# The work beside the experts begins at rank 16 in place of 4 and ends at 59, and until rank 16 five more places hold loaded weights

## The chip, the core and the metric

The kernel runs on one core of a Trainium2 chip. The metric is the device time of one execution in microseconds (us). A core has TensorE (PE in the profile; PEld is its weight load), VectorE (DVE), ScalarE (ACT), GpSimd (POOL) and SyncE (SP), each with its own queue of instructions that it takes in order, and 16 DMA engines that all queues share.

## The reference, cut to what matters

One decoder layer for 520 tokens (512 of a prompt, 8 samples), 1024 wide, in float32. The part that the change touches is the mixture of experts: 64 experts, each token goes to 8 of them, beside them a shared expert and a gated per-layer input.

```python
def moe(x, w):
    scores = sigmoid(xf @ w_router);  top 8 of scores + router_bias;  gates = 2.5 * top_s / sum(top_s)
    for each expert e, for its tokens tok with gates g:
        h = silu(xb @ w1[e]) * (xb @ w3[e])          # 1024 -> 256
        acc[tok] += (h @ w2[e]) * g                  # 256 -> 1024
    shared = (silu(xf @ ws1) * (xf @ ws3)) @ ws2
    return acc + shared

x  = layer_norm(ALPHA * x + mixer(x))
ff = moe(x, w)
ple = sigmoid(x @ w_ple_gate) * (p_l @ w_ple)
x  = layer_norm(ALPHA * x + ff + ple)
```

## The kernel before, in words

The first third of the program is the mixer (projections, state-space branch, attention); the change doesn't touch it. `second_phase` then does the first norm, the router, and the experts.

**Ranks.** The router sorts the experts by load; rank 0 is the first expert handled, and `CAPS` gives the most rows of each rank, from 112 down to 56. The loop `for e in range(NE + 1)` (L1597) handles one rank a turn. It issues the input product of rank e (`expert_in`, 24 matmuls of 512 columns), the transposes of the rows of rank e+1 (`turn`), the output product of rank e-1 (`expert_out`, 12 matmuls of 512 columns, then the gate on ScalarE, L1448, and a scatter that adds the rows into one of two sums in DRAM, L1449), and `fetch(e + 3)`: the row numbers of rank e+3 and the gather of its rows (L1412). Odd ranks below 58 add into the second sum (`accD` with the higher number in the order), all others into the first. At the end of rank 60 and 61 `second_sums` (L1374) adds the second sum to the residual by five accumulating DMAs that GpSimd issues.

**Weights.** An expert's weights are six pieces of 512 KB. `Stream.load_to` (L307) issues their DMAs on SyncE (L318) in the order in which they are used, into places for loaded weights: a piece takes a place until it has been split. `Stream.split_to` splits it into a high part (ScalarE, L269, `hi`) and a rest (`lo`, L265, on VectorE, on GpSimd for one piece in six). A product then takes three matmuls: high by high, high by rest, rest by high. There are seven places for good (`raw2`, tag "raw2", RAW2 = 7). `stream.use(n, ...)` says from which piece on which pool gives the places. Until rank 4 pieces also go to five places of the pool `pre` (PRE = 5), in turns of seven and five.

**The work beside the experts.** The list `side` (L1595) has 39 steps: six for the second half of the shared expert's input (`shared_more`), six for its output (`shared_out`), four times six for the per-layer input (`layer_inputs`: a step that loads weights, then one of 30 matmuls of 256 columns for each of five tiles of tokens), and three for the last norm's scales. Their tiles are named `x` (the PSUM bank), `ph`, `pl` (the split weights), `praw` (the one place into which these weights are loaded, L1313 on SyncE) and `pt`. They need the pool `pw`, which is opened where `pre` is closed (L1618 to L1620). The `while` (L1621) says at which rank a step is issued: step n when (e - 4) * 39 / 52 reaches n, so from rank 6 to 56.

**Order.** Within this the order on each engine is the program's own scheduler's: it moves instructions between neighbouring steps as far as their tiles allow.

Of the kernel before, what the change touches and what calls it, by code (L numbers as in the profile page):

```python
# [46 lines left out]
RAW2 = 7  # L47
YB = 2
PRE = 5
VB = 5  # L50
N_SIDE = 39
SECOND = 58
SIDE = N_SIDE / 52
N_DENSE = 54
assert len(CAPS) == NE

# [144 lines left out]
def trunk_step(ctx: ExitStack, tc: tile.TileContext, I, O):  # L201
# [29 lines left out]
    def open_pool(*a, **k):  # L231
        cm = pool(*a, **k)
        p = cm.__enter__()
        opened.append((p, cm))
        return p
# [109 lines left out]
    P2 = 48  # L345
# [26 lines left out]
    stream = Stream(srcs)  # L372
# [364 lines left out]
    side = []  # L737
# [536 lines left out]
    def shared_mid(out, hg):  # L1274
        S.activation(hg, out[:, 0:128], AF.Silu)
        mul(V, hg, hg, out[:, 128:256])
        return hg

    def shared_turn(hg, i, c):

        ps = bank()
        T.transpose(ps[:, 0:TT], hg, ident[0:TT, 0:TT])
        split(H['shared'][:, i, 0, c], H['shared'][:, i, 1, c], ps[:, 0:TT])

    def shared_in():

        pair = [mm2(), mm2()]
        outs = [pair[i // 2][0:TT, i % 2] if i < 4 else psx.tile([128, 512], F32, tag="x", name="x")[0:TT] for i in R5]
        outs = [o[:, 0:256] for o in outs]
        for q in range(2):  # L1290
            hi, lo = (t.rearrange("p (k n) -> p k n", k=4) for t in stream.get(P2 + q, 0))
            for i in R5:
                yield from shared_product(outs[i], i, hi, lo, range(4 * q, 4 * q + 4), 4 * q)
        H['first half'] = outs
# [111 lines left out]
    def fetch(e):  # L1406
        find(e)
        gather(e)
# [18 lines left out]
    def expert_in(e):  # L1427
        ps, m = bank(), CAPS[e]
        for q in range(4):
            hi, lo = (t.rearrange("p (k n) -> p k n", k=2) for t in stream.get(AT[e] + q))  # L1430
            ffn_in(ps[0:m], *XT[e], hi, lo, q, slice(0, m))
        HG[e] = ffn_mid(ps, m)
        XT.pop(e)
# [41 lines left out]
    def second_phase():  # L1475
# [5 lines left out]
        raw2 = open_pool("raw2")  # L1481
# [69 lines left out]
        moe = open_pool("moe", side="right")  # L1551
        stream.use(P2, None, (moe, "v", VB))
        pre = open_pool("pre", side="right")
        stream.use(P2 + RAW2, (pre, "pre", PRE))
        stream.use(P2 + RAW2 + PRE, (raw2, "raw2", RAW2))
        stream.use(P2 + 2 * RAW2 + PRE, (pre, "pre", PRE))
        stream.use(P2 + 2 * RAW2 + 2 * PRE, (raw2, "raw2", RAW2))
        filler = shared_in()

        def fill(n):  # L1560
# [34 lines left out]
        side = [(q, i) for q in range(-2, 4) for i in range(-1, 5)]  # L1595
        side += [(4, -1), (4, 0), (4, 1)]
        for e in range(NE + 1):  # L1597
            if e == NE - 1:
                last_rows()
            if 0 < e < NE:  # L1600
                expert_in(e)
            if 0 < e < NE - 1:
                turn(e + 1)
            if e:
                expert_out(e - 1)
            else:
                H['shared'] = py.tile([128, 5, 2, 2, TT], F32R, tag="side", name="st")
                mids = py.tile([MAX_CAP, 1024], F32, tag="y", bufs=YB, name="mids")
                mids = [shared_mid(H['first half'][i], mids[0:TT, 128 * i:128 * i + 128]) for i in R5]
            if 0 < e < 6:  # L1610
                shared_turn(mids[e - 1], e - 1, 0)
            if 0 < e < NE - 1:
                HT[e] = ffn_turn(HG.pop(e), CAPS[e])
            if e + 3 < NE:
                fetch(e + 3)
            for i in {SECOND + 2: (0, 1, 2), SECOND + 3: (3, 4)}.get(e, ()):
                second_sums(i)
            if e == 4:  # L1618
                close_pool(pre)
                pw = open_pool("pw")  # L1620
            while side and (e - 4) * SIDE >= N_SIDE - len(side) + 1:  # L1621
                q, i = side.pop(0)
                if q == -2:
                    shared_more(i)
                elif q == -1:
                    shared_out(i)
                elif q < 4:
                    layer_inputs(q, i)
                else:
                    last_scales(i)  # L1630
# [66 lines left out]
    def last_rows():  # L1697

        yy = pw.tile([128, 2, 1024], F32R, tag="pl", name="yy")
        H['yh'], H['yl'] = yy[:, 0], yy[:, 1]  # L1700
        to = H['to'] = pw.tile([128, 5, TT], F32R, tag="praw", name="to")
        G.memset(yy.bitcast(F32), 0.0)
        G.memset(to.bitcast(F32), 0.0)
        for e in (NE - 2, NE - 1):
            m, z = CAPS[e], 64 * (NE - 1 - e)
            oh = OH.pop(e)
            for tiles in ((0, 1, 2), (3, 4)):
                ps = mm2()[:, 0]
                for n, i in enumerate(tiles):
                    T.matmul(ps[z:z + m, TT * n:TT * n + TT], lhsT=oh[:, i], rhs=ident_b[0:TT, 0:TT], start=True, stop=True)  # L1710
                a, b = tiles[0], tiles[-1] + 1
                S.activation(to[z:z + m, a:b], ps[z:z + m, 0:TT * len(tiles)].rearrange("p (i t) -> p i t", t=TT), AF.Copy)
# [116 lines left out]
    close_pool(gpool)  # L1829
    close_pool(qkv)  # L1830
    second_phase()


# [16 lines left out]
```

## Time and profile before

| what | value |
|---|---|
| median of three runs | 1328.86 us (1328.29 to 1329.45) |
| profiled execution: time, span | 1326.8 us, 1325.1 us |
| busy in the span: PE, DVE, ACT, POOL | 1188.6, 939.5, 700.4, 535.2 us |
| expert ranks 4 to 62 | 504.21 to 1284.94 us |

The profile is of one execution. Its span runs from the first to the last instruction. A rank is counted here from the start of its SiLU on ScalarE (L1254, the tile `hg`) to that of the next rank; the stretches in the rows are cut at these starts, which are 504.21 us for rank 4, 677.04 for rank 16, 855.59 for rank 29, 1156.44 for rank 54, 1237.15 for rank 60 and 1284.94 for rank 63. Matmuls are pipelined: a row's duration is longer than the distance to the next start, which is what a matmul costs in a stream of them. The DMA share is the busy share of the 16 DMA engines, and q1 is the queue of the weights, q0 that of the gathers, scatters and accumulating DMAs.

### The profile page before, as it was taken

To read this page: it belongs to the slowest core of one execution; us is meant where nothing else is said; L and a number is where in the kernel's file an instruction comes from. 1 tells how busy PE (TensorE), PEld (TensorE's weight loads), DVE (VectorE), ACT (ScalarE), POOL (GpSimd) and SP (SyncE) were. 2 spreads that over 40 slices of the span, in tenths; PEclk is the share of its full clock that TensorE was granted. 3 is DMA by queue.
4 is the path that set the end of the run, shared out by engine and by line. 5 is a ranking of instruction groups with operands and counts; after the bars stand their busy time and mean duration, and the time that the engine had idled before them with its cause. 6 is when DMAs were issued, how large, how long until landed. Compare 5 with 4: busy or idle time off the path is not lost. (4 is left out here: it accounts for less than half of the span.)

```text
span 1325.1 us, 20407 instructions
## 1 busy us (share of the span) xinstructions
PE 1188.6 (90%) x7083; PEld 887.7 (67%) x7084; DVE 939.5 (71%) x1397; ACT 700.4 (53%) x1055; POOL 535.2 (40%) x327
## 2 busy tenths in 40 slices
PE   7699999999998979888899888899999999988683
PEld 7699799899877856556566566667666666644341
DVE  7974657833468778576779566788877887766566
ACT  4131535222213566566567556677767776766462
POOL 1822141011124446343656335454554544455325
PEclk9897899999997989888999889999999999989897
DMA  8476563253343699889989978999999999979973
GB/s 295 124 255 114 188 202 121 83 143 96 112 149 103 196 266 252 255 264 294 310 253 322 299 232 280 286 335 318 332 319 309 335 318 293 291 254 279 256 218 93
DMA packets 114236, 312.93 MB, mean 236 GB/s; under 512 B 37041, under 2 KB 37465, under 8 KB 113055
## 3 DMA queue, kind: packets, MB, share of 16 engines
q1 hardware_dynamic: 68307, 247.11, 54.8%
q0 software_dynamic: 30848, 43.33, 15.0%
q10 hardware_dynamic: 14974, 21.14, 6.0%
q8 instruction: 57, 0.93, 0.3%
q14 instruction: 50, 0.41, 0.1%
HBM read 276.32 MB, written 32.87 MB: 233 GB/s over the span
## 5 line engine op out<-in xcount | busy, mean ns | idle before, releaser
L265 DVE TENSOR_TENSOR lo<-raw,hi 128x1024 fp32r<-128x1024 f32 x371 | 519.1, 1410 | 197.9 <-ACT hi L269 193.2
L269 ACT ACTIVATE hi<-raw 128x1024 fp32r<-128x1024 f32 x434 | 450.4, 1055 | 259.6 <-DMA raw<-in_we_dram 107.2
L1449 POOL DMA_INDIRECT accD<-y,idx x62 | 127.4, 2054 | 283.0 <-ACT hh L269 146.9
L210 PE MATMUL a<-hi,xgh 128*64 128x512 f32 (+18 forms) x512 | 212.7, 415 | 7.0 <-ACT hi L269 4.8
L210 PE MATMUL a<-lo,xgh 128*64 128x512 f32 (+18 forms) x512 | 210.8, 412 | 5.2 <-DVE lo L265 5.0
L210 PE MATMUL a<-hi,xgl 128*64 128x512 f32 (+18 forms) x512 | 207.6, 405 | 0.0
L265 POOL TENSOR_TENSOR lo<-raw,hi 128x1024 fp32r<-128x1024 f32 x63 | 169.7, 2694 | 54.2 <-ACT hi L269 45.2
L1412 POOL DMA_INDIRECT xg<-xD,idx x64 | 114.1, 1783 | 104.6 <-DVE idx L1394 43.2
L210 PE MATMUL mm<-xh,hi 128*128 128x260 f32 (+1 forms) x576 | 120.5, 290 | 18.9 <-DVE r L259 10.5
L210 PE MATMUL mm<-xl,hi 128*128 128x260 f32 (+1 forms) x576 | 119.1, 288 | 0.7 <-DVE xl L265 0.7
L210 PE MATMUL mm<-xh,lo 128*128 128x260 f32 (+1 forms) x576 | 119.1, 288 | 0.0
L210 PEld LDWEIGHTS a<-hi,xgh 128*64 128x64 f32 (+18 forms) x512 | 75.9, 148 | 51.8 <-ACT hi L269 8.5
L210 PEld LDWEIGHTS a<-lo,xgh 128*64 128x64 f32 (+18 forms) x512 | 76.1, 149 | 45.2 <-DVE lo L265 10.4
L210 PEld LDWEIGHTS mm<-xh,hi 128*128 128x128 f32 x576 | 91.3, 193 | 19.8 <-issue 10.8
L210 PEld LDWEIGHTS a<-hi,xgl 128*64 128x64 f32 (+18 forms) x512 | 75.6, 148 | 38.4 <-issue 4.5
L210 PE MATMUL mm<-lo,hh 128*64 128x512 f32 (+18 forms) x256 | 86.2, 419 | 15.1 <-POOL lo L265 12.5
L210 PEld LDWEIGHTS mm<-xl,hi 128*128 128x128 f32 x576 | 91.0, 193 | 1.3 <-DVE xl L265 1.0
L210 PE MATMUL mm<-hi,hh 128*64 128x512 f32 (+18 forms) x256 | 85.5, 416 | 7.1 <-ACT hi L269 6.7
L210 PEld LDWEIGHTS mm<-xh,lo 128*128 128x128 f32 x576 | 91.2, 193 | 0.1
L1448 ACT ACTIVATE y<-mm,both 78x1024 f32<-78x1024 f32 (+19 forms) x62 | 68.7, 1107 | 36.1 <-PE mm L210 33.0
L210 PE MATMUL mm<-hi,hl 128*64 128x512 f32 (+18 forms) x256 | 83.6, 409 | 0.0
L215 PEld LDWEIGHTS a<-ident,xg 64*128 64x128 f32 (+18 forms) x512 | 50.9, 146 | 43.1 <-issue 16.8
(410 smaller groups left out, 1971.4 us busy)
## 6 DMA issues: line engine op xcount, KB each, us to landing
raw<-in_we_dram SPq DMA_DIRECT2D x384, 512.0 KB
raw<-in_wd_dram SPq DMA_DIRECT2D x50, 512.0 KB
accD<-zeros_b POOLq DMA_DIRECT2D x2, 2560.0 KB
praw<-in_wp_dram SPq DMA_DIRECT2D x8, 512.0 KB
base<-in_xtok_dram ACTq DMA_DIRECT2D x1, 2080.0 KB
xD<-base ACTq DMA_DIRECT2D x5, 416.0 KB
base<-accD POOLq DMA_DIRECT2D x5, 416.0 KB
acc<-accD SPq DMA_DIRECT2D x5, 416.0 KB
```

What stands on the lines that cost most here:

```text
L210: ins = nc.tensor.matmul(*a, **k)
L215: ins = nc.tensor.transpose(*a, **k)
L265: return e.tensor_tensor(out=o, in0=a, in1=b, op=ALU.subtract)
L269: a = S.activation(hi, src, AF.Copy)
L1412: G.indirect_dma_start(out=XG[e % 3][0:m], out_offset=None, in_=xD[:, :], in_offset=bass.IndirectOffsetOnAxis(ap=IX[e][0:m, 0:1], axis=0), ...
L1448: S.activation(y.rearrange("p (h n) -> p h n", h=2), ps[0:m], AF.Copy, scale=GC.pop(e)[0:m])
L1449: G.indirect_dma_start(out=sumsD[e % 2 if e < SECOND else 0][:, :], out_offset=bass.IndirectOffsetOnAxis(ap=IX.pop(e)[0:m, 0:1], axis=0), ...
```

## The change

Three things. The steps of `side` are issued from rank 18 to 59: step n when (e - 16) * 39 / 43 reaches n. The pool `pre` is closed, and `pw` opened, at rank 16. And the turns of seven and five places go on until then: pieces 55, 67, 79, 91, 103, 115 and 127 each begin five in `pre`, where before only the first two did; from piece 132 on all go to `raw2`. Since a line is added ahead of it, lines L53 to L1553 have numbers higher by one in the changed kernel.

```diff
-SIDE = N_SIDE / 52
+ALONE = 16
+SIDE = N_SIDE / 43
...
-        stream.use(P2 + RAW2, (pre, "pre", PRE))
-        stream.use(P2 + RAW2 + PRE, (raw2, "raw2", RAW2))
-        stream.use(P2 + 2 * RAW2 + PRE, (pre, "pre", PRE))
-        stream.use(P2 + 2 * RAW2 + 2 * PRE, (raw2, "raw2", RAW2))
+        for n in range(P2 + RAW2, P2 + 6 * ALONE - PRE, RAW2 + PRE):
+            stream.use(n, (pre, "pre", PRE))
+            stream.use(n + PRE, (raw2, "raw2", RAW2))
...
-            if e == 4:
+            if e == ALONE:
                 close_pool(pre)
                 pw = open_pool("pw")
-            while side and (e - 4) * SIDE >= N_SIDE - len(side) + 1:
+            while side and (e - ALONE) * SIDE >= N_SIDE - len(side) + 1:
```

What this moves on TensorE, at rank 5 (92 rows). Before, the rank's output product (`mm`) is followed by the first step of the side work, matmuls from `ph` and `pl` into `x`:

```order
L210 MATMUL mm<-hi,hl 94x512 x2
L215 MATMUL a<-ident,mids 128x104
L210 MATMUL x<-ph,x1h 104x256
L210 MATMUL x<-pl,x1h 104x256
L210 MATMUL x<-ph,x1l 104x256
```

In the changed kernel the next rank's input product (88 rows) follows at once:

```order
L211 MATMUL mm<-hi,hl 94x512 x2
L211 LDWEIGHTS oh
L211 MATMUL x<-what,oh 84x6
...
L216 MATMUL a<-ident,mids 128x104
L216 MATMUL a<-ident,hg 128x92 x2
L211 MATMUL a<-hi,xgh 88x512
L211 MATMUL a<-lo,xgh 88x512
```

So the 24 matmuls of that step are gone from rank 5. The number of side matmuls by rank follows from the same order (36 matmuls of 512 columns belong to each rank itself). Ranks 4 to 15: 120 of 256 columns and 12 of 512 before, none now. Ranks 16 to 28: 150 of 256 and 48 of 512 before; 120 and 24 now. Ranks 29 to 53: 450 of 256 before; 480 of 256 and 36 of 512 now, in columns as much as 552 of 256. Ranks 54 to 59: four of 512 before; 120 of 256 and two of 512 now. On SyncE the first load of side weights stands behind 29 expert loads before, behind 89 now.

What moves on GpSimd near the end of the experts. Before, the five accumulating DMAs of the second sum (L1374) come behind the gathers of the last two ranks (the last `xg` row) and behind the scatter of rank 57 (`accD_148`) and that of rank 58 (`accD_147`):

```order
L1412 DMA xg_4187<-xD,idx 56x1024
L1449 DMA accD_147<-y,idx 640x1024
L265 TENSOR_TENSOR lo<-raw,hi 128x1024
L1412 DMA xg_4189<-xD,idx 56x1024
L1449 DMA accD_148<-y,idx 640x1024
L1412 DMA xg_4185<-xD,idx 56x1024
L265 TENSOR_TENSOR lo<-raw,hi 128x1024
L1449 DMA accD_147<-y,idx 640x1024
L1374 DMA base<-accD_148 104x1024 x5
```

In the changed kernel they come right behind the scatter of rank 57, ahead of the scatter of rank 58 and of the gather of rank 62; the gather of rank 63 is the last row here:

```order
L1450 DMA accD_148<-y,idx 640x1024
L266 TENSOR_TENSOR lo<-raw,hi 128x1024
L1375 DMA base<-accD_148 104x1024 x5
L1450 DMA accD_147<-y,idx 640x1024
L266 TENSOR_TENSOR lo<-raw,hi 128x1024
L1413 DMA xg_4189<-xD,idx 56x1024
L1702 MEMSET yy 128x2048
L266 TENSOR_TENSOR lo<-raw,hi 128x1024
L1450 DMA accD_147<-y,idx 640x1024
L1413 DMA xg_4185<-xD,idx 56x1024
```

So the five accumulating DMAs moved ahead of one scatter and of the gathers of the last two ranks, which stood ahead of them.

## Rows read from the trace of the kernel before

**Rows 1.** The page: busy times, then tenths of the span's 40 slices.
```profile
PE 1188.6 (90%) x7083; PEld 887.7 (67%) x7084; DVE 939.5 (71%) x1397; ACT 700.4 (53%) x1055; POOL 535.2 (40%) x327
...
PEclk9897899999997989888999889999999999989897
DMA  8476563253343699889989978999999999979973
```

**Rows 2.** Stretches by rank: busy us (instructions), granted clock, DMA share.
```profile
core 0: us, PE busy (x) PEld busy (x) DVE busy (x) ACT busy (x) POOL busy (x), PEclk, DMA share, GB/s
504.21:677.04 172.83, 148.41 (x771) 102.92 (x770) 123.33 (x166) 103.31 (x147) 82.61 (x38) 0.91 0.90 276
677.04:855.59 178.55, 158.87 (x856) 107.22 (x855) 131.61 (x180) 113.27 (x153) 82.33 (x40) 0.94 0.92 285
855.59:1156.44 300.85, 295.26 (x1711) 197.62 (x1710) 247.63 (x334) 216.17 (x299) 152.62 (x75) 1.00 0.99 317
1156.44:1237.15 80.71, 71.18 (x325) 36.27 (x325) 52.23 (x71) 49.35 (x70) 41.32 (x21) 0.94 0.85 266
1237.15:1284.94 47.79, 36.67 (x141) 17.72 (x142) 28.36 (x27) 25.39 (x37) 16.18 (x11) 0.82 0.83 235
```

**Rows 3.** DMA, 504.21 to 677.04: packets, MB, share of 16 engines; then issues.
```profile
q1 hardware_dynamic: 10742, 39.13, 65.8%
q0 software_dynamic: 7325, 8.37, 23.4%
...
raw<-in_we_dram SPq DMA_DIRECT2D x72, 512.0 KB
praw<-in_wd_dram SPq DMA_DIRECT2D x2, 512.0 KB
praw<-in_wp_dram SPq DMA_DIRECT2D x1, 512.0 KB
```

**Rows 4.** DMA, 855.59 to 1156.44, in the same columns.
```profile
q1 hardware_dynamic: 22840, 82.40, 78.7%
q0 software_dynamic: 7820, 12.56, 19.9%
...
raw<-in_we_dram SPq DMA_DIRECT2D x151, 512.0 KB
praw<-in_wp_dram SPq DMA_DIRECT2D x4, 512.0 KB
praw<-in_wp_dram SPq DMA_DIRECT2D x3, 256.0 KB
```

**Rows 5.** Timeline, ScalarE: the SiLU of ranks 0 and 3.
```profile
455.64 0.39 ACT L1254 ACTIVATE hg<-a 112x256 f32<-112x256 f32 x1 [0.47 <-PE a L210]
...
484.39 0.38 ACT L1254 ACTIVATE hg<-a 100x256 f32<-100x256 f32 x1 [0.33 <-PE a L210]
```

**Rows 6.** Timeline, TensorE in rank 46: start, duration.
```profile
1062.10 0.40 PE L210 MATMUL a<-hi,xgl 128*64 128x512 f32 x1
1062.33 0.39 PE L210 MATMUL a<-hi,xgh 128*64 128x512 f32 x1
...
1063.25 0.28 PE L210 MATMUL x<-ph,pTs 128*104 128x256 f32 x1
1063.37 0.28 PE L210 MATMUL x<-pl,pTs 128*104 128x256 f32 x1
```

**Rows 7.** Timeline, TensorE in rank 3: a wait for gathered rows.
```profile
492.39 1.49 PE L215 MATMUL a<-ident,xg 94*128 94x94 f32 x8 [7.85 <-DMA xg<-xD,idx]
```

**Rows 8.** The stretch around that wait, columns as in rows 2.
```profile
486.70:496.90 10.20, 4.51 (x16) 3.69 (x17) 3.83 (x8) 1.32 (x3) 1.07 (x1) 0.50 0.82 217
```

**Rows 9.** Timeline, GpSimd: scatters of ranks 57 and 58, the second sum.
```profile
1217.64 2.13 POOL L1449 DMA_INDIRECT accD<-y,idx  x1 [2.41 <-ACT hh L269]
...
1228.46 2.13 POOL L1449 DMA_INDIRECT accD<-y,idx  x1 [4.05 <-ACT hh L269]
1236.82 4.46 POOL L1374 DMA_DIRECT2D base<-accD  x5 [6.23 <-DMA accD<-y,idx]
```

## The prediction

> **What bounds the kernel now.** I read the page first, then a table of stretches by rank, then the DMA queues of two stretches, then the timeline at single places. On the page TensorE is busy for 90% of the span and the DMA tenths are 8 or 9 in nearly all slices of the experts, the last twenty-six or so [rows 1]. So two things are near their limit there. The table by rank parts them [rows 2]. In ranks 29 to 53 the DMA engines are busy for 0.99 of 300.85 us, the granted clock is 1.00 (2.4 GHz throughout), and TensorE is busy for 295.26: both are full. In the other stretches neither is. Ranks 4 to 15 have a DMA share of 0.90, ranks 16 to 28 of 0.92, ranks 54 to 59, which have almost no side work, of 0.85, ranks 60 to 62 of 0.83, and the clock is between 0.82 and 0.94 there, so TensorE spent part of each at 1.2 GHz.
>
> Since all expert weights have to come in, the time of the experts is the DMA work plus the time in which the DMA engines stand idle. The idle time is 0.10 x 172.83 = 17 us in ranks 4 to 15, 0.08 x 178.55 = 14 in 16 to 28, 3 in 29 to 53, 0.15 x 80.71 = 12 in 54 to 59, 0.17 x 47.79 = 8 in 60 to 62, 54 us in all [rows 2]. The change adds no transfer and takes none away; it can only move this idle time.
>
> What a full place costs is seen at rank 3: TensorE waits 7.85 us for gathered rows [rows 7], and around it the clock is 0.50, TensorE busy for 4.51 of 10.20 us [rows 8]. While TensorE stands or runs at half speed, loaded weights aren't split, the places fill, and SyncE cannot issue the next load.
>
> **The change, stretch by stretch.** All sums go against the profiled execution (1326.8 us, span 1325.1), 2.1 us under the median of 1328.86.
>
> *Ranks 4 to 15.* Out go 120 side matmuls of 256 columns and 12 of 512. A matmul of 512 columns costs 0.23 us, one of 256 costs 0.12 [rows 6], so 17 us of TensorE. What is left is far from filling it: ranks 0 to 2 took 484.39 - 455.64 = 28.75 us, 9.6 a rank, with weights loaded ahead [rows 5], so twelve ranks need 115 us. The DMA work is the floor: q1 moved 75 loads in 0.658 x 172.83 = 113.7 us, 1.52 us a load, and q0 took 0.234 x 172.83 = 40.4 us [rows 3]. Three loads were side weights; in the changed kernel's order the first three stand behind 89, 96 and 103 expert loads, so most still fall at the end of this stretch. With 72 to 74 loads the work is 109 + 40 + 1 = 150 to 153 us. How much idle time comes on top decides. Twelve places hold two ranks of weights in place of one and a sixth, so a stop of TensorE of some us no longer stops the loads; against it, TensorE has nothing to do between weights. No row shows twelve places in a long stretch without side work. The bounds are the shares of the nearest rows: 0.85 as in ranks 54 to 59, which gives 150/0.85 = 177 us (4 more than now), and 0.99 as in ranks 29 to 53, which gives 152 (21 less). I take 0.94, between the 0.90 that the stretch has now and 0.99: 160 us, a gain of 13.
>
> *Ranks 16 to 28.* Side columns fall from 150 + 2 x 48 = 246 matmuls of 256 to 120 + 2 x 24 = 168, 9 us of TensorE, which isn't full here. This stretch begins with the step from twelve places to seven, which before fell at rank 4: five loads, 7.6 us of DMA time, that the first stretch could do ahead and this one can not. I take a gain of 2; bounds: share 0.85 in place of 0.92 (15 longer) and 0.99 (13 shorter).
>
> *Ranks 29 to 53.* Here the cover is gone: both engines are full. Side matmuls rise from 450 to 552 of 256 columns: 102 x 0.12 = 12.2 us of TensorE. Side loads rise from 4 + 3 halves to 8 + 4 halves and the one of the tokens' inputs, 5.5 loads of 1.51 us (0.787 x 300.85 = 236.8 us over 156.5 loads [rows 4]): 8.3 us of DMA. The two overlap, so the loss is not their sum. Bounds: 5 if the DMA share goes to 1.00, 16 if TensorE's 12.2 come whole and its waits grow. I take 10.
>
> *Ranks 54 to 59.* 120 matmuls of 256 columns come in, two of 512 go: 14 us of TensorE, no loads. The DMA work is 0.85 x 80.71 = 68.6 us. With side work as dense as in ranks 29 to 53 TensorE doesn't run dry; at the 12.4 us a rank that the line above gives (310.85/25), six ranks take 74.6. I take a gain of 5; bounds 69 (all DMA, 12 shorter) and 95 (the 14 us come on top).
>
> *Ranks 60 to 62 and the end.* In the order on GpSimd the five DMAs of the second sum move ahead of the scatter of rank 58 and of the gathers of ranks 62 and 63. They now begin at 1236.82, after 6.23 us of waiting, 17 us behind the end of the scatter of rank 57 [rows 9]. If that scatter lands no earlier, GpSimd stands for longer, and the gather of rank 62 queues behind five transfers of 416 KB. Nothing else is queued there but one split of GpSimd and the scatter of rank 58, for which a `y` place waits. The stretch has 8 us of idle DMA to lose it in. I take a loss of 3, bounds 0 and 10. The last norm is untouched.
>
> Sum: -13 - 2 + 10 - 5 + 3 = -7 us: 1319.8 in the profiled execution, 1321.9 on the scale of the median. I forecast 1322.
>
> **The rivals.**
>
> *A: the clock decides (slower).* The mechanism: TensorE needs 9.6 of the 12.5 us that a rank's DMA takes, so it waits in every rank from 4 to 15, falls to 1.2 GHz, and then needs up to twice as long for the next weights; the places fill at last, twelve as well as seven. For it: each stretch with a clock under 0.95 has a DMA share under 0.93, the stretch with the least side work (54 to 59) has 0.85, and the only stretch at clock 1.00 is the one in which side work fills TensorE [rows 2]. Against it: five more places are 7.6 us of loads, more than the 5 us of work that 10 us at half clock lose [rows 8]. The price: 177 us in ranks 4 to 15 (+4), 2 lost in 16 to 28, then +10, -5, +3: +14, 1343. It decides from a DMA share of 0.89 on in ranks 4 to 15, where the gain there falls under 5 us and the sum turns.
> The Trainium skill has this as a rule (TensorE: Matmul & The Clock Gate, section "HAM oscillation — how this bites in real kernels"): where a tile's matmuls are shorter than the wait for the next operand, TensorE goes back to half clock at every tile, and the remedy is to keep it fed. The clocks of 0.91 to 0.94 against 1.00 bear it out here, and by it the time would be rival A's.
>
> *B: it comes out even.* The DMA share of ranks 4 to 15 stays at 0.90 in spite of the places, since the stops are waits for gathers, as at rank 3, where twelve places were there already and did not help [rows 7]. Then the stretch takes 151/0.90 = 168 (-5), and the rest sums to +6: 1329 to 1330.
>
> *C: the gain is whole.* Ranks 4 to 15 reach 0.98 (154 us, -19), ranks 16 to 28 gain 7 with a quieter start, ranks 29 to 53 lose only 8, ranks 54 to 59 gain 8, the end nothing: -26, 1303. For it: every idle us of the DMA engines in ranks 4 to 15 is one in which places were full.
>
> *D: the change does less than it says.* The scheduler could leave side steps where they were or SyncE could stand behind a side load. The order excludes the first: no side matmul is left in ranks 4 to 15. For the second, the first side load stands behind 89 expert loads, not 29, so a stop of SyncE behind it would come at rank 14 and cost what it costs at rank 3 now.
>
> **How the numbers follow.** The forecast 0.38, with a range of its own from 1312 to 1326; C 0.18; B 0.16; A 0.28; D has no chance of its own. A measurement of this kernel tells about 0.2%, 2.7 us, from no change: faster is under 1326.2, slower above 1331.5. Forecast and C are faster: 0.56. B is the same: 0.16. A is slower: 0.28. The range reaches from C's 1303 to a little short of A's 1343: 1303 to 1341.
>
> **What would show it.** Right: a DMA share of 0.93 or more in ranks 4 to 15 and about 160 us for them; ranks 29 to 53 some 10 us longer at clock 1.00; ranks 54 to 59 at a clock near 1.00 and 75 us. Wrong: a clock under 0.88 in ranks 4 to 15 with a share under 0.89 (A); more than 16 us lost in ranks 29 to 53, which would mean that TensorE, not the loads, sets the pace there; a wait of TensorE for the gather of rank 62 of over 10 us.

## The result, and the profile after

The changed kernel takes 1385.19 us (median of four runs, 1382.68 to 1387.70) against 1329.15 us for the kernel before beside it: ratio 1.0405, 95% interval 1.0371 to 1.0438. It is 56 us slower; forecast was 1322, 7 us faster, with a range up to 1341. Its profiled execution took 1382.68 us with a span of 1380.8.

The page after, in the columns of [rows 1]:

```profile
PE 1191.6 (86%) x7082; PEld 892.5 (65%) x7084; DVE 951.2 (69%) x1397; ACT 702.6 (51%) x1055; POOL 525.8 (38%) x327
...
PEclk9899999999997989888899988999999999999886
DMA  7478653532514889886799987997899999878963
```

TensorE is busy for as long as before (1191.6 us against 1188.6), the granted clock is a little lower, and the DMA tenths show 6, 7 and 8 where they were 9. So the work is the same and the time beside it has grown. Where, is in the windows of the changed kernel, cut at the SiLU of ranks 0, 4, 16, 29, 41, 54, 60 and 63, in the columns of [rows 2]:

```profile
456.63:509.14 52.51, 39.35 (x211) 29.83 (x210) 38.19 (x54) 33.00 (x46) 22.29 (x12) 0.87 0.89 263
509.14:686.64 177.50, 135.22 (x661) 88.92 (x661) 121.82 (x159) 100.53 (x137) 81.70 (x38) 0.88 0.84 255
686.64:863.40 176.76, 150.94 (x784) 100.71 (x782) 126.63 (x161) 112.08 (x156) 77.30 (x37) 0.93 0.90 282
863.40:1034.95 171.55, 152.67 (x842) 104.39 (x843) 124.44 (x169) 107.20 (x149) 80.96 (x36) 0.91 0.87 275
1034.95:1205.63 170.68, 167.00 (x964) 110.84 (x963) 139.25 (x185) 115.00 (x159) 74.35 (x40) 0.99 0.93 294
1205.63:1290.04 84.41, 78.29 (x408) 47.87 (x408) 59.36 (x76) 51.22 (x70) 28.34 (x15) 0.96 0.81 251
1290.04:1341.87 51.83, 34.79 (x150) 18.41 (x149) 25.33 (x30) 25.67 (x40) 23.04 (x15) 0.80 0.79 207
```

[Rows 2] gave 172.83, 178.55, 300.85, 80.71 and 47.79 us for ranks 4 to 15, 16 to 28, 29 to 53, 54 to 59 and 60 to 62. The third of these is two windows here, so that two causes can be told apart; before they were:

```profile
455.64:504.21 48.57, 39.86 (x214) 30.21 (x212) 39.04 (x55) 33.79 (x47) 22.56 (x11) 0.89 0.84 244
...
855.59:1001.36 145.77, 140.68 (x847) 98.67 (x846) 122.08 (x166) 105.71 (x147) 76.79 (x37) 1.00 1.00 322
1001.36:1156.44 155.08, 154.58 (x866) 98.95 (x865) 125.55 (x169) 110.46 (x153) 75.83 (x39) 1.00 0.98 312
```

So the loss is +3.9 us in ranks 0 to 3, +4.7 in 4 to 15, -1.8 in 16 to 28, **+25.8 in 29 to 40, +15.6 in 41 to 53**, +3.7 in 54 to 59, +4.0 in 60 to 62. Three places carry the explanation, and the end is a fourth, smaller one.

**Ranks 41 to 53: TensorE.** Here the changed kernel's TensorE is busy for 167.00 of 170.68 us at clock 0.99 while the DMA share falls to 0.93. The start of the SiLU of ranks 44, 45 and 46 (timeline, ScalarE: start, duration) shows what a rank costs without and with a step of side work:

```profile
1073.89 0.37 ACT L1255 ACTIVATE hg<-a 66x256 f32<-66x256 f32 x1
1083.70 0.38 ACT L1255 ACTIVATE hg<-a 64x256 f32<-64x256 f32 x1 [0.52 <-PE a L211]
1097.37 0.38 ACT L1255 ACTIVATE hg<-a 64x256 f32<-64x256 f32 x1
```

Rank 44 has no side matmul and takes 9.81 us, rank 45 has a step of 30 and takes 13.67. Before, the loads set 300.85/25 = 12.03 us a rank, and a step stood in about every second rank. Now ten of these thirteen ranks have one. Ten ranks at 13.67 and three at 9.81 make 166 us, 13 ranks of loads at 12.03 make 156: TensorE sets the pace.

**Ranks 29 to 40: a bunch and late rows.** Three steps of side work, 90 matmuls, fall into rank 35. Two of them, 60 matmuls, follow each other on TensorE from 944.15 to 952.83 with no expert's matmul between. Then TensorE stands 4.06 us for gathered rows, those of rank 36, and the third step comes at 965.72, inside the next input product. GpSimd had issued the gather of these rows only at 944.16 (timelines of TensorE and GpSimd; the idle time before an instruction and what ended it in brackets):

```profile
952.83 0.28 PE L211 MATMUL x<-ph,x1l 128*104 128x256 f32 x1
957.17 1.17 PE L216 MATMUL a<-ident,xg 68*128 68x68 f32 x8 [4.06 <-DMA xg<-xD,idx]
...
965.72 0.28 PE L211 MATMUL x<-ph,pTs 128*104 128x256 f32 x1
...
944.16 4.49 POOL L1413 DMA_INDIRECT xg<-xD,idx  x1 [3.16 <-DVE idx L1395]
```

The gather is late because the search for the rows is late: the index of rank 36 is written at 943.64, when rank 35 already runs, and before it was written while rank 31 ran (888.46). The matmuls of the search go to the same bank `x` as the side work, and stood behind a step that TensorE worked off in pieces from 909.32 to 933.52. ScalarE meanwhile splits no weights from 946.4 to 962.94 (timeline; `pt` belongs to the side work, `hi` is an expert's split):

```profile
945.37 1.05 ACT L270 ACTIVATE hi<-raw 128x1024 fp32r<-128x1024 f32 x1
947.88 0.38 ACT L1355 ACTIVATE pt<-x 104x256 f32<-104x256 f32 x1 [1.46 <-PE x L211]
953.15 0.39 ACT L1355 ACTIVATE pt<-x 104x256 f32<-104x256 f32 x1 [4.89 <-PE x L211]
957.92 0.85 ACT L270 ACTIVATE xgh<-a 128x272 fp32r<-128x272 f32 x2 [4.39 <-PE a L216]
```

No split means no free place, and the loads stop. Two windows, the two steps with the wait, and the stretch behind them:

```profile
944.15:957.50 13.35, 8.11 (x69) 7.62 (x68) 5.33 (x10) 2.83 (x4) 9.68 (x4) 0.91 0.92 295
957.50:966.00 8.50, 8.31 (x41) 5.47 (x40) 3.73 (x9) 3.41 (x6) 1.15 (x1) 0.74 0.20 60
```

The DMA share falls to 0.20, and rank 35 takes 29.05 us (941.58 to 970.63).

**Ranks 4 to 15: one late scatter stops three engines.** The timeline of GpSimd, VectorE, ScalarE and TensorE:

```profile
580.64 3.55 POOL L1450 DMA_INDIRECT accD<-y,idx  x1 [4.30 <-ACT y L1449]
...
614.21 0.21 DVE L1395 TENSOR_SCALAR idx<-both,slots 78x1 int32<-78x1 f32 x1 [9.94 <-DMA accD<-y,idx]
...
614.21 1.11 ACT L1449 ACTIVATE y<-mm,both 84x1024 f32<-84x1024 f32 x1 [10.25 <-DMA accD<-y,idx]
...
615.60 0.72 PE L211 MATMUL a<-lo,xgh 128*82 128x512 f32 x1 [9.56 <-DVE lo L266]
```

The scatter of rank 8, issued at 580.64, lands 33.5 us later. VectorE is about to write the row numbers (`idx`, eight tiles used in turn) of rank 16 into the tile that this scatter still reads, and waits; behind it in VectorE's queue stand the splits `lo`, and TensorE waits for those. Around it:

```profile
604.00:614.20 10.20, 2.04 (x12) 1.22 (x10) 0.27 (x1) 0.00 (x0) 0.00 (x0) 0.81 0.63 223
614.20:622.00 7.80, 4.15 (x15) 2.46 (x16) 5.58 (x7) 3.71 (x5) 5.11 (x3) 0.50 0.67 175
```

The clock is 0.81 while TensorE stands and 0.50 after it: here the wait comes first and the clock follows. The sums of such waits over ranks 4 to 15 (view of waits: engine, line, for what: us in total, times, longest; SPq is SyncE, which issues the loads):

```profile
DVE idx L1395 <- DMA accD<-y,idx: 25.8, 3, 10.0
...
PE a L211 <- DVE lo L266: 17.9, 3, 9.6
...
SPq L319 <- DVE idx L1395: 15.3, 2, 13.7
```

Before, VectorE had no such wait in this stretch. The index of rank 16 was written there without one, while rank 13 ran (its SiLU is at 633.24):

```profile
638.81 0.20 DVE L1394 TENSOR_SCALAR idx<-both,slots 78x1 int32<-78x1 f32 x1
```

In the changed kernel it is due while rank 11 runs. Counted from the rank whose SiLU came last, the index was written three or four ranks ahead in ranks 12 to 15 before, and is written five or six ahead now: the side work had held the search back.

**The end** went as the prediction said. GpSimd's timeline, and TensorE's wait for gathered rows:

```profile
1272.24 2.13 POOL L1450 DMA_INDIRECT accD<-y,idx  x1 [0.30 <-issue]
...
1290.19 4.49 POOL L1375 DMA_DIRECT2D base<-accD  x5 [13.38 <-DMA accD<-y,idx]
1294.98 2.17 POOL L1450 DMA_INDIRECT accD<-y,idx  x1 [0.30 <-issue]
...
1299.75 1.04 POOL L1413 DMA_INDIRECT xg<-xD,idx  x1 [0.21 <-issue]
...
1320.70 1.07 PE L216 MATMUL a<-ident,xg 56*128 56x56 f32 x8 [6.77 <-DMA xg<-xD,idx]
```

The second sum waits 13.38 us in place of 6.23 [rows 9], the gather behind it is issued at 1299.75, and TensorE stands 6.77 us for it.

### The profile page after: what moved, and what is told of

Its sections match the earlier page's. It is cut to its first block, busy times and chain, and to the rows that moved or that the text cites. A ratio compares the mean times of both kernels' runs of the same rounds, so it can differ in the third digit from the quotient of the medians.

```text
span 1380.8 us, 20358 instructions
## 1 busy us (share of the span) xinstructions
PE 1191.6 (86%) x7082; PEld 892.5 (65%) x7084; DVE 951.2 (69%) x1397; ACT 702.6 (51%) x1055; POOL 525.8 (38%) x327
## 5 line engine op out<-in xcount | busy, mean ns | idle before, releaser
L266 DVE TENSOR_TENSOR lo<-raw,hi 128x1024 fp32r<-128x1024 f32 x371 | 534.0, 1456 | 158.0 <-ACT hi L270 151.9
L1450 POOL DMA_INDIRECT accD<-y,idx x62 | 132.3, 2134 | 360.6 <-ACT y L1449 230.8
L211 PE MATMUL a<-lo,xgh 128*64 128x512 f32 (+18 forms) x512 | 211.9, 414 | 18.0 <-DVE lo L266 17.9
L266 POOL TENSOR_TENSOR lo<-raw,hi 128x1024 fp32r<-128x1024 f32 x63 | 173.4, 2752 | 33.3 <-ACT hi L270 25.3
L1413 POOL DMA_INDIRECT xg<-xD,idx x64 | 100.2, 1565 | 104.9 <-DVE idx L1395 44.8
L211 PEld LDWEIGHTS mm<-xh,hi 128*128 128x128 f32 x576 | 93.0, 197 | 27.8 <-issue 17.4
L211 PEld LDWEIGHTS a<-hi,xgh 128*64 128x64 f32 (+18 forms) x512 | 76.3, 149 | 52.2 <-issue 7.0
L216 PE MATMUL a<-ident,xg 64*128 64x64 f32 (+18 forms) x512 | 58.3, 247 | 51.7 <-DMA xg<-xD,idx 51.7
L211 PE MATMUL mm<-hi,hh 128*64 128x512 f32 (+18 forms) x256 | 89.0, 426 | 7.9 <-ACT hi L270 7.3
L1449 ACT ACTIVATE y<-mm,both 78x1024 f32<-78x1024 f32 (+19 forms) x62 | 68.9, 1111 | 52.4 <-DMA accD<-y,idx 30.4
## 6 DMA issues: line engine op xcount, KB each, us to landing
base<-accD POOLq DMA_DIRECT2D x5, 416.0 KB, 10.5
```

Of the source, the lines that this page charges most:

```text
L211: ins = nc.tensor.matmul(*a, **k)
L216: ins = nc.tensor.transpose(*a, **k)
L266: return e.tensor_tensor(out=o, in0=a, in1=b, op=ALU.subtract)
L1413: G.indirect_dma_start(out=XG[e % 3][0:m], out_offset=None, in_=xD[:, :], in_offset=bass.IndirectOffsetOnAxis(ap=IX[e][0:m, 0:1], axis=0), ...
L1449: S.activation(y.rearrange("p (h n) -> p h n", h=2), ps[0:m], AF.Copy, scale=GC.pop(e)[0:m])
L1450: G.indirect_dma_start(out=sumsD[e % 2 if e < SECOND else 0][:, :], out_offset=bass.IndirectOffsetOnAxis(ap=IX.pop(e)[0:m, 0:1], axis=0), ...
```

## The experiments

The theories in the first eight: P, the side work is too dense in the late ranks and TensorE sets the pace there; Q, twelve loads under way make gathers and scatters late; R, the stops come from the loads of side weights through their one place; C, TensorE without side work falls to half speed. In the later seven: S, the index's wait is what costs in ranks 4 to 15, against T, the wait only moves; R2, the bunch at rank 35, against G, gathers and scatters land late whatever the order.

Ratios are to the kernel before on the same chip. Stretches are us of the profiled execution, by ranks.

| kernel | median us | ratio, 95% | 0-3 | 4-15 | 16-28 | 29-40 | 41-53 | 54-62 |
|---|---|---|---|---|---|---|---|---|
| before | 1329.15 | | 48.6 | 172.8 | 178.6 | 145.8 | 155.1 | 128.5 |
| changed | 1385.19 | 1.0371-1.0438 | 52.5 | 177.5 | 176.8 | 171.6 | 170.7 | 136.2 |
| e1_late_side | 1386.08 | 1.0395-1.0443 | 46.6 | 189.5 | 177.0 | 164.2 | 169.5 | 136.1 |
| e2_after_thin | 1357.01 | 1.0161-1.0228 | 54.4 | 178.0 | 179.7 | 154.5 | 157.8 | 130.5 |
| e3_end59 | 1333.36 | 0.9983-1.0038 | 48.4 | 168.8 | 176.0 | 148.1 | 161.4 | 127.8 |
| e4_before_thin | 1348.25 | 1.0080-1.0177 | 45.6 | 172.9 | 189.6 | 148.6 | 156.7 | 130.9 |
| e5_from10 | 1361.78 | 1.0176-1.0277 | 53.3 | 169.2 | 179.2 | 149.2 | 173.3 | 136.8 |
| e6_after_warm | 1404.22 | 1.0502-1.0615 | 52.4 | 194.9 | 178.9 | 168.3 | 171.7 | 137.3 |
| e8_one_load | 1379.77 | 1.0329-1.0421 | 51.3 | 177.1 | 179.9 | 166.5 | 167.7 | 135.8 |
| e9_before_warm | 1358.66 | 1.0188-1.0264 | 50.6 | 188.5 | 179.1 | 150.0 | 157.3 | 138.4 |
| e10_after_idx | 1379.65 | 1.0311-1.0392 | 52.2 | 164.9 | 183.4 | 173.1 | 168.4 | 137.9 |
| e11_late_idx | 1380.59 | 1.0301-1.0389 | 46.7 | 180.7 | 179.1 | 164.6 | 169.5 | 138.9 |
| e12_before_idx | 1329.35 | 0.9970-1.0018 | 48.6 | 172.6 | 179.5 | 147.8 | 155.6 | 127.1 |
| e13_from10_idx | 1356.89 | 1.0146-1.0219 | 54.6 | 163.8 | 179.4 | 149.1 | 172.4 | 137.1 |
| e14_even | 1379.94 | 1.0274-1.0408 | 54.7 | 177.8 | 178.8 | 159.5 | 169.3 | 141.8 |
| e15_even_idx | 1364.47 | 1.0202-1.0285 | 52.3 | 163.1 | 182.2 | 159.5 | 171.8 | 139.3 |
| e16_from6 | 1338.92 | 1.0032-1.0072 | 47.2 | 179.4 | 176.6 | 148.9 | 165.6 | 123.3 |

**e1_late_side.** The late side work, but only seven places from piece 72 on, as before:

```diff
-        for n in range(P2 + RAW2, P2 + 6 * ALONE - PRE, RAW2 + PRE):
+        for n in range(P2 + RAW2, P2 + 2 * (RAW2 + PRE), RAW2 + PRE):
```

> The side work from rank 18 to 59 as in the changed kernel, but only seven places for loaded weights from piece 72 on, as before. Theory P (the side work is packed too densely; in ranks 29 to 53 TensorE sets the pace): the late ranks stay as slow as in the changed kernel, 1375 to 1388 us. Theory Q (twelve loads under way make gathers and scatters wait, and their lateness is what costs): ranks 4 to 15 fall from 177 to 165 us or less and the total to 1370 or less. Theory C (the clock: without side work TensorE falls to half speed, and fewer places make that worse): ranks 4 to 15 take over 185 us, total over 1390.

The whole is the same as the changed kernel, as P said. Ranks 4 to 15 take 12 us more without the five places, where Q expected them to fall; C's bound for them (over 185) is met, its bound for the whole is not. Ranks 0 to 3 take 6 less. VectorE waits for old scatters even longer, its waits in ranks 4 to 15:

```profile
DVE idx L1395 <- DMA accD<-y,idx: 47.1, 6, 12.5
```

Q has something in ranks 0 to 3 only: the nine kernels with twelve places take 51 to 55 us there, those with seven 46 to 49 (51 in e9, which has added matmuls). In ranks 29 to 53, where the loss is large, all kernels have seven places; yet this one takes 333.7 us there and the changed kernel 342.2. With the same work the stretch so varies by some 9 us from kernel to kernel, and a difference of that size says nothing.

**e2_after_thin** and **e4_before_thin.** The changed kernel and the kernel before, each without the third product of the per-layer inputs (200 of 600 matmuls of 256 columns, 24 us of TensorE; the term rest by high is left out):

```diff
-                for l, w in ((xs[0], H['ph']), (xs[0], H['pl']), (xs[1], H['ph'])):
-                    T.matmul(o, lhsT=l[:, k, c], rhs=w[:, k0 + k], start=(n == 0), stop=(n == 3 * kn - 1))
+                for l, w in ((xs[0], H['ph']), (xs[0], H['pl'])):
+                    T.matmul(o, lhsT=l[:, k, c], rhs=w[:, k0 + k], start=(n == 0), stop=(n == 2 * kn - 1))
```

> The changed kernel with the third product (rest of the input by high part of the weights) left out of the per-layer inputs: 200 matmuls of 256 columns fewer in ranks 34 to 57, 24 us of TensorE at 0.12 us each; loads, splits and waits stay. Theory P: at least the 24 us go, 1345 to 1361 us, as nearly all of the loss sits in the matmuls. Theory R (the stops come from the side work's loads through one place and from bunched steps, not from the amount of matmuls): under 10 us go, 1375 or more.

> The kernel before with the same third product left out of the per-layer inputs: 200 matmuls of 256 columns fewer in ranks 22 to 52. If the loads set the pace in ranks 29 to 53 of the kernel before, under 5 us go (1324 to 1329), or it gets slower, since TensorE then runs dry there too. If TensorE sets the pace there, 15 to 24 us go (1305 to 1314).

Ranks 29 to 53 of the changed kernel, of e2 and of e4, in the columns of [rows 2]:

```profile
863.40:1205.63 342.23, 319.67 (x1802) 215.23 (x1803) 263.69 (x353) 222.20 (x307) 155.31 (x76) 0.95 0.90 285
```

```profile
868.48:1180.78 312.30, 290.79 (x1637) 191.54 (x1637) 266.46 (x353) 221.64 (x308) 160.71 (x76) 0.98 0.96 307
```

```profile
866.08:1171.42 305.34, 285.92 (x1553) 179.50 (x1552) 236.17 (x335) 213.67 (x299) 155.95 (x77) 0.99 0.98 307
```

In the changed kernel 165 fewer matmuls there bring 30 us: 20 by their own 0.12 each, the rest in fewer stops (rank 35 alone takes 20.82 us in place of 29.05). In the kernel before 158 fewer bring nothing (305 against 301), at a DMA share of 0.98. P holds: TensorE's work sets the pace in the changed kernel's late ranks and did not before. That e4 as a whole became slower comes for the most part from ranks 16 to 28, 11 us longer, in which VectorE now waits for old scatters as in the changed kernel's ranks 4 to 15 (0.9 us in the kernel before):

```profile
DVE idx L1394 <- DMA accD<-y,idx: 21.3, 3, 9.0
```

**e3_end59.** The kernel before with its side work spread to rank 59:

```diff
-SIDE = N_SIDE / 52
+SIDE = N_SIDE / 55
```

> The kernel before, with the side work spread to rank 59 in place of 56 (39 steps over 55 ranks in place of 52); it still begins at rank 4. Side matmuls in ranks 29 to 53 fall from 450 to as much as 420 of 256 columns, in 54 to 59 they rise from 8 to 64. Theory P: 29 to 53 gain about 4 us and 54 to 59 lose nothing, 1318 to 1326 us. Theory C (side work where TensorE runs dry keeps its clock): the same sign, more of it in ranks 54 to 59. If where the side work ends does not matter: 1327 to 1331.

No difference that can be measured, so P's forecast of 1318 to 1326 was missed: ranks 29 to 53 have fewer side matmuls and take 309.6 us against 300.9. To end at rank 59 is not by itself what costs.

**e5_from10.** The changed kernel with the side work counted from rank 10 (its first step falls into rank 12), and the twelve places until there:

```diff
-ALONE = 16
-SIDE = N_SIDE / 43
+ALONE = 10
+SIDE = N_SIDE / 49
```

> The changed kernel with the side work from rank 10 in place of 16 (still ending at 59), the twelve places until rank 10. In its order ranks 4 to 9 hold no side matmuls, 10 to 15 as much as 24 of 256 columns, 29 to 53 as much as 378 (450 before, 552 in the changed kernel). Theory P (too many side matmuls in ranks 29 to 53 cost the 41 us there): 29 to 53 are back at 305 us or less, and the total at 1325 to 1345. Theory R (stops at the start of the per-layer inputs, whatever the amount): 29 to 53 stay over 320, total over 1350. Theory C (TensorE without side work loses its clock) adds 5 to 10 us in ranks 4 to 15 against the kernel before, in either case.

It lies between the two. Ranks 29 to 53 take 322.5 us, which meets R's bounds (over 320, over 1350 in all) and misses P's (305 or less). Ranks 29 to 40, without a bunch, are nearly back (149.2), ranks 41 to 53 are not (173.3). There 270 side matmuls fall, against 216 before and 300 in the changed kernel, but the stretch is 2.6 us longer than the changed kernel's: TensorE is idle for 9.1 us of it, against 3.7. So the number of matmuls alone doesn't give the time there.

**e6_after_warm** and **e9_before_warm.** The changed kernel with 16 added matmuls of 256 columns, whose result isn't used, in each of ranks 4 to 15, and the kernel before with the same in ranks 3, 4 and 56 to 61:

```diff
+        ps = psx.tile([128, 512], F32, tag="x", name="x")[0:TT, 0:256]
+        for k in range(n):
...
+            if e in range(4, 16):
+                warm(16)
```

> The changed kernel with 16 matmuls of 256 columns more in each of ranks 4 to 15, whose results nothing reads: 192 matmuls, 23 us of TensorE. Theory C (without side work TensorE falls to 1.2 GHz between loads, and this costs more than the work): ranks 4 to 15 get shorter in spite of it, 165 to 172 us in place of 177.5, clock 0.92 or more. If gathers and scatters or loads set the pace there (theory Q): 175 to 182, no gain. If TensorE's work sets it: 190 to 200.

> The kernel before with 16 matmuls of 256 columns more in each of ranks 3, 4 and 56 to 61, which hold no side work; nothing reads their results: 128 matmuls, 15 us of TensorE. Theory C: the ranks 54 to 62, 128.5 us now at clocks of 0.94 and 0.82, get 5 to 12 us shorter, total 1316 to 1325. If the clock there follows from waits for loads and gathers that the extra work doesn't touch: the same, 1327 to 1333, or up to 10 longer.

Both make ranks 4 to 15 longer, by 17.4 and 15.6 us, at a lower clock (0.85 for 0.88, 0.88 for 0.91). In e9 ranks 54 to 62, where C expected 5 to 12 us less, take 9.9 more. TensorE's waits in ranks 4 to 15, e6 and then e9:

```profile
PE a L216 <- DMA xg<-xD,idx: 44.5, 4, 17.0
```

```profile
PE a L215 <- DMA xg<-xD,idx: 34.5, 3, 15.1
```

The added matmuls did not keep TensorE at full speed: it stood for gathered rows instead. They are no clean test of C, though, since they are written into `x`, the bank of the search. In e6 the index is written three ranks ahead in ranks 5 to 15, in the changed kernel four to six, so the gathers start later; and no wait of VectorE for an old scatter is left (25.8 us in the changed kernel). That work between the ranks holds the search back is seen here from the other side. C is not borne out, and not excluded.

**e8_one_load.** The changed kernel with the per-layer weights loaded once and used for all four quarters (three of four quarters are computed with the wrong weights):

```diff
         if i < 0:
+            if q:
+                return
```

> The changed kernel with the weights of the per-layer inputs loaded and split once in place of four times (all four quarters computed with the first quarter's weights): nine loads, nine splits and the waits for their one place are gone, all matmuls stay. Theory R (stops from those loads): ranks 29 to 53 fall from 342 us to 320 or less. Theory P (matmuls): they stay at 332 or more, since only 11 us of DMA time go, where TensorE sets the pace.

Ranks 29 to 53 take 334 us in place of 342, and R's 320 is missed. But e1 and e11, which keep all side loads, take 334 there too, so no part of the loss is shown to be theirs.

**e10_after_idx**, **e11_late_idx**, **e12_before_idx**, **e13_from10_idx.** The changed kernel, e1, the kernel before and e5, each with an own column for every rank's index, so that VectorE's write waits for no scatter:

```diff
-            IX[e] = moe.tile([128, 1], I32, tag="idx", bufs=8, name="idx")
+            if 'idx' not in H:
+                H['idx'] = moe.tile([128, 64], I32, tag="idx", bufs=1, name="idx")
+            IX[e] = H['idx'][:, e:e + 1]
```

> The changed kernel with one edit: the index of every rank has a column of its own in one tile of 64 columns, in place of eight tiles that are used in turn. VectorE's write of an index so waits for no scatter; the order of TensorE's work is the same but for 7 rows. Theory S (in ranks 4 to 15 the index write of rank e, which waits for the scatter of rank e-8 to land, holds VectorE's queue, behind it the splits, TensorE and the loads): VectorE's waits of 25.8 us there go, TensorE's 17.9 us for VectorE's splits with them, ranks 4 to 15 fall from 177.5 us to 155 to 165, the whole to 1363 to 1373. Rival T (the software queue is late whatever waits for it): the wait moves to ScalarE's products, which wait for the same scatters to give back their y (22.2 us now), or to TensorE's gathered rows; ranks 4 to 15 stay at 173 to 180 and the whole at 1380 to 1390. Both: ranks 29 to 53 stay at 335 to 345 us, since TensorE sets the pace there.

> The kernel with the late side work but seven places from piece 72 on as before (which took 1386.08 us, ranks 4 to 15 at 189.5, VectorE's index waiting 47.1 us there), with a column of its own for every rank's index. Theory S: ranks 4 to 15 fall to 158 to 170 us, and the whole to 1358 to 1370, as fast as the changed kernel with the same edit or faster: then the five more places were worth only the wait that they hid. Rival T: 182 to 190 us there and 1378 to 1388 in all. A middle result, 172 to 178 there, would say that the wait for the index took the 12 us between this and the changed kernel and the places nothing beyond.

> The kernel before with a column of its own for every rank's index. In its ranks 4 to 15 VectorE hardly waits for an old scatter, since the side work stands between; both theories expect little. S: 1323 to 1329 us, ranks 4 to 15 at 168 to 173 (the few us of waits for the index and what follows them). T: 1327 to 1333, the same as before.

> The kernel with the side work from rank 10 to 59 (1361.78 us, ranks 4 to 15 at 169.2 with 17.1 us of VectorE's waits for old scatters), with a column of its own for every rank's index. S: ranks 4 to 15 at 155 to 163 us, the whole at 1348 to 1356. T: 166 to 171 there, 1358 to 1365 in all. Neither expects it under the kernel before, since ranks 41 to 53 hold 270 side products of 256 columns against 216 and keep their 173 us.

In e10 ranks 4 to 15 fall from 177.50 to 164.85 us, within what S expected; TensorE's waits there are now

```profile
PE x L211 <- DVE both L1392: 9.4, 2, 8.1
PE a L216 <- DMA xg<-xD,idx: 8.9, 2, 4.8
...
PE a L211 <- DVE lo L266: 1.3, 2, 1.0
```

The 17.9 us for VectorE's splits are 1.3; a part came back as a wait for another of VectorE's results, `both`, which itself waits for ScalarE's `y`, and that for a scatter. But S was wrong on the whole: 6.7 us are given back in ranks 16 to 28 (183.43 against 176.76), nearly all of it at rank 16 itself (18.26 against 11.89), and two more expert loads now fall there (81 against 79; 66 against 68 in ranks 4 to 15). The profiled executions differ by 1.3 us, the medians by 5.5, and the intervals of the ratios overlap. In e11 ranks 4 to 15 gain 9 of the 20 to 30 us that S expected and lie between all the ranges named for them, in e13 they gain 5.4, and in the kernel before, which has no such wait, nothing. So S is right on the wait; that half of its 12.6 us moved on to rank 16, and little is seen at the end, is T's side.

**e14_even** and **e15_even_idx.** The changed kernel with a pace at which no two steps stand together on TensorE, and the same with the index's columns of e10:

```diff
-SIDE = N_SIDE / 43
+SIDE = N_SIDE / 42.5
```

> The changed kernel with a pace of 39 steps over 42.5 ranks in place of 43: the same matmuls, loads and places, but on TensorE no two steps of side work stand together any more (ranks 33 to 38 hold 18, 30, 30, 30, 30 and 0 matmuls of 256 columns in its order, where the changed kernel's have 12, 12, 6, 90, 30 and 0 one rank further on). Theory R2 (the bunch holds TensorE for 11 us, no weights are split meanwhile, the places are full, SyncE stops loading for 12 us, and TensorE stands afterwards): ranks 29 to 53 fall from 342 us to 326 to 334, the whole from 1385 to 1370 to 1378. Rival G (gathers and scatters land late whatever the order): ranks 29 to 53 at 338 to 346 and the whole at 1380 to 1390. Both: ranks 41 to 53 stay at 167 to 173, since TensorE sets the pace there.

> The changed kernel with the pace of 42.5 ranks and a column of its own for every rank's index. If the two causes add up (R2 and S): 5 us less than the even pace alone, 1365 to 1373 in all, ranks 4 to 15 at 165. G: 1374 to 1384.

Ranks 29 to 40 of e14, to be read against 863.40:1034.95 of the changed kernel, and ranks 29 to 53:

```profile
866.85:1026.30 159.45, 147.44 (x872) 103.30 (x872) 127.35 (x172) 107.67 (x150) 70.06 (x37) 0.97 0.92 294
...
866.85:1195.58 328.73, 310.63 (x1802) 209.96 (x1801) 268.74 (x355) 221.50 (x308) 147.49 (x77) 0.98 0.92 294
```

With 30 matmuls more in ranks 29 to 40 they take 12.1 us less, and ranks 29 to 53 with the same number of matmuls 13.5 less, within R2's bounds. That the crowded rank costs is shown: rank 35 takes 12.7 us in e14 and e15, and 23.9 to 29.6 in the changed kernel, e1, e8, e10 and e11, which have 842 matmuls each in ranks 29 to 40. How much is less sure. These five take 164.2 to 173.1 us there, e14 and e15 159.5, so it is 5 to 14 us. And the edit moved two things: with the two steps apart, the index of rank 36 is written three ranks ahead in place of one, so the bunch and the late rows are not told apart. Of the whole only 5.2 us appear, with overlapping intervals (R2 expected 7 to 15, and the runs scatter from 1365 to 1381); ranks 60 to 62, 4.3 us longer, and ranks 0 to 3, 2.2 longer, take most of the rest in the profiled execution. Both edits together bring 20.7 us, more than the 5.2 and the 5.5 of each alone, and only this difference is clear of the intervals.

**e16_from6.** A version drawn from this, out of the changed kernel: side work counted from rank 6 over 50 ranks (steps in ranks 8 to 56), the five places on the same pieces as in the kernel before, the index's columns of e10.

```diff
-ALONE = 16
-SIDE = N_SIDE / 43
+ALONE = 6
+SIDE = N_SIDE / 50
```

> A version drawn from the reasons: side work from rank 6, 39 steps over 50 ranks (the last ends at rank 56, ahead of the second sum as before), the five more places on the same pieces as before but their pool kept until rank 6, a column of its own for every rank's index. By the price of a side matmul the late ranks lose 2 to 4 us to the denser pace, ranks 4 to 15 gain 4 to 9 from fewer of them and from the index. If only that counts: 1321 to 1327. If the stops decide, which every other placement has moved about: 1327 to 1342, not faster than before.

It is 0.5% slower than before. The end is shorter (123.3 us for ranks 54 to 62 against 128.5), ranks 41 to 53 are 10.5 us longer with 270 side matmuls for 216 (54 at 0.12 are 6.5), and ranks 4 to 15 are 6.6 longer. No version of the study is faster than the kernel before.

## Why the prediction was wrong, step by step

*Ranks 29 to 53, forecast +10 with bounds 5 and 16, measured +41.4: the step that failed.* The term for TensorE's work was right in size: 12.2 us for 102 matmuls; the trace has some 108 more there, 13 us at 0.12 each [rows 6]. What failed is the sentence that both engines are full and that their losses overlap, and with it the upper bound, which left about 4 us for TensorE's waits to grow. By the rows TensorE is idle for 22.6 us of the stretch against 5.6, 17 us more, and busy for 24.4 us more, of which 13 are the added matmuls and the other 11 or so go with a granted clock of 0.95 for 1.00. The prediction's own sign of error was over 16 us lost, and it said what that would mean: TensorE, not the loads, sets the pace. That is so in ranks 41 to 53, where TensorE is busy for 167.00 of 170.68 us: 84 matmuls more make 10 us of the 15.6. It is only half so in ranks 29 to 40. There some 24 more make 3 of 25.8 us; TensorE's idle time grows from 5.1 to 18.9 us and the clock falls from 1.00 to 0.91. 5 to 14 us of that go with what e14 changed, the crowded rank 35 above all; its three steps stood in the order of the changed kernel and could have been read there. The rest is open. One stop is seen at rank 33 (19.6 us), where TensorE waits 4.1 us for a split of GpSimd, which stands behind a scatter that holds GpSimd for 8.84 us. The side loads are not shown to be part of it (e8).

*Ranks 4 to 15, forecast -13, measured +4.7.* The share taken was 0.94, the measured one 0.84, just under the lower bound. The step that failed: "a stop of TensorE of some us no longer stops the loads". The stops were 10 us long and not TensorE's: VectorE stood for an old scatter, so nothing was split and SyncE, with twelve places as well, stood for VectorE. Without that wait the stretch takes 164.85 us, near the 160 forecast, but half of the gain comes back as a loss at rank 16. The prediction asked what TensorE would do without the side work, not what the side work had held apart.

*Ranks 16 to 28, forecast -2, measured -1.8.* The number is right. No run separates the two terms that it was made of, and a wait that moves over rank 16 changes it by 6.7 us (e10), so the close agreement is in part luck.

*Ranks 54 to 59, forecast -5, measured +3.7.* The mechanism held in part: TensorE is idle for 6.1 us in place of 9.5, at clock 0.96 against 0.94. But the DMA share fell from 0.85 to 0.81 where it was to rise. The size was taken from the line that failed: 12.4 us a rank where ranks 29 to 53 turned out at 342.23/25 = 13.7; six ranks at that make 82, measured 84.4.

*Ranks 60 to 62, forecast +3, measured +4.0.* Right, by the mechanism named: the second sum waits longer, and the gather behind it is late by 6.77 us, under the 10 that would have been a sign of error.

*Ranks 0 to 3, not in the forecast, +3.9.* The nine kernels with twelve places are all longer there than the others; by what way, no run shows.

*The rivals.* A gave 1343 by 177 us and a lower clock in ranks 4 to 15. Its 177 was hit (177.50, clock 0.88), its cause is not borne out: the longest stops are waits for scatters, and without them e10 takes 12.65 us less at nearly the same clock (0.89). The rule of the Trainium skill that the prediction weighed there (TensorE: Matmul & The Clock Gate, section "HAM oscillation — how this bites in real kernels") says that TensorE falls back to half clock where the wait for the next operand is longer than the work on a tile. The trace agrees on what is seen: a granted clock of 0.50 behind a wait of 9.56 us. As a remedy the section names a loop that does the work of several tiles ahead of each wait, so that TensorE's clock stays up, or more rows a tile; no run here does that, since the added matmuls of e6 left it waiting 44.5 us for gathered rows. B's reason, that the stops are waits for DMAs that more places don't help, came nearest, but it named gathers where scatters were the greater part, and priced the late ranks at the prediction's own +10. D's second half, side weights in one place, is not shown to cost anything (e8).

Summed: of 56 us ranks 29 to 53 hold 41, the end from rank 54 on 8, ranks 4 to 15 5 and ranks 0 to 3 4; ranks 16 to 28 give 2 back. Of the 41, 13 are TensorE's denser work and 5 to 14 go with the crowded rank 35; 14 to 23 are open. e15, which takes away the crowded rank and the index's wait, still stands 34 us above the kernel before, 30 of them in ranks 29 to 53.

## What to carry to other kernels

Where two engines are both full, price moved filler on each of them, in stretches of a few units of the loop, and take the longer sum (here 166 us for TensorE in ranks 41 to 53 against 156 for the loads); that both were full before doesn't mean that the losses overlap. Then ask what single stops add, which a sum doesn't show: here they and the lower clock cost more than the work itself. Before work is taken out of a stretch, look at what it holds apart: the scheduler moves up what stood behind it, here an index write that reuses a tile which a slow scatter still reads, and an in-order queue turns that one wait into a stop of three engines. Read the new order for steps that now stand together, and for small steps, here the search for a rank's rows, that share a bank with the filler and now come late.

## What was not expected of the hardware

An accumulating scatter landed 33.5 us after its issue (580.64 to 614.21) with weights loading beside it, more than three times the 9.8 us of a rank's own work; the median of the twelve scatters in ranks 4 to 15 was 19.7 us, that of the 25 from 860 to 1200 us was 8.0. And less work was slower: 200 matmuls less in the kernel before gave a ratio of 1.0129 (1.0080 to 1.0177), 128 more, some 15 us, gave 1.0226 (1.0188 to 1.0264); in both the largest new waits are not for matmuls but for the DMAs of scatters (21.3 us of VectorE's) and gathers (34.5 us of TensorE's), each in one stretch.
